# Sums of weight blocks formed by accumulating transfers instead of by VectorE additions

## The chip, the core and the metric

The kernel runs on one core of a Trainium2 chip. The core has a matrix engine (TensorE, "PE" in the profile, with its weight loads as "PEld"), a vector engine (VectorE, "DVE"), a scalar engine (ScalarE, "ACT"), GpSimd ("POOL") and SyncE ("SP"). In this kernel SP and POOL do little besides starting transfers: each has a queue of its own, works through it in order, and an entry that has to wait for something holds up all that stand behind it. The metric is the device time of one execution in microseconds (us).

## The reference

Two layers of a decoder trunk on 512 positions of width 1024, all in float32: dilated sliding-window attention, then a gated recurrent block, each followed by a gated convolutional feed-forward block. What matters here is one product of the attention layer, the values of groups 1 and 2:

```python
def dilated_attention_mixer(x, w_qkv, w_o, rel_bias):
    B, S, _ = x.shape
    qkv = (x @ w_qkv).reshape(B, S, N_GROUPS, 3, HEADS_PER_GROUP, HEAD_DIM)
    outs, lses = [], []
    for g in range(N_GROUPS):
        tbl = rel_bias[:, g * HEADS_PER_GROUP:(g + 1) * HEADS_PER_GROUP]
        o, lse = dilated_group_attention(qkv[:, :, g, 0], qkv[:, :, g, 1], qkv[:, :, g, 2],
                                         tbl, WINDOWS[g], DILATIONS[g])
```

`x` here is the normalised input, 512 x 1024, and `w_qkv` is 1024 x 9216. The bias of each head comes from a table `rel_bias` by distance.

## The kernel before

**Numbers.** A float32 product is made of three passes of TensorE: each operand is split into a high part (`hi`, rounded) and a rest (`lo = raw - hi`), and hi·hi, hi·lo and lo·hi are added up in PSUM.

**Weights.** All weights come through one list, `plan`, in the order of use. `load` (L243) starts the transfer of an entry into one of three buffers named `raw`, mostly 1 MB, on SP's queue. `pump` (L187) takes an entry apart into two units, ScalarE writes `whi` (L215) and VectorE writes `wlo` (L226, or L165 in the first entries). At most eight units may be ready or in use (`W_UNITS`). `loads` (L239) starts further entries while fewer than three buffers are unread. After each stretch of matrix work the program calls `tick`, which lets `pump` make one or two units and advances the side jobs (softmax, bias tables and the like). So on each engine the order is that of one Python program written in the order of TensorE's work; nothing reorders it later.

**Seven products.** The value projection of groups 1 and 2 is made, twice (for head pairs 0 and 1, and for 2 and 3), by seven products of half-size blocks instead of eight. Four of the seven need a sum of weight blocks as one operand. Let W(i, f) be the block of 512 rows i and 512 columns f. The list holds, for each of the two rounds, the blocks W(0,0) and W(1,0); then a first sum A = W(0,0) + W(0,1); B = A + W(1,1); C = B + W(1,0); then W(1,1) alone; then D = W(0,1) + W(1,1). Between these stand the weights of the query and key projections (`w_cols`). The entries of a sum are called `held` and `sum0` (both blocks of a fresh sum) or `sum` (one block added to the last sum):

```python
            [q("value", 0, 0), q("value", 1, 0)],
            [q("held", 0, 0), q("sum0", 0, 1)],
            [q("sum", 1, 1)],
            [q("sum", 1, 0)],
            [q("value", 1, 1)],
            [q("held", 0, 1), q("sum0", 1, 1)],
```

All go through `raw` buffers. `added` (L230) adds on VectorE, half a block at a time, into a tile `sum` that shares the place of the tile `gain` (the norms' gains); then the halves of `sum` are split into `whi` and `wlo` like any other weight. A block has 1024 column pieces of 1 KB each: 128 partitions, four rows of each, two groups' columns.

**POOL's queue.** POOL's queue carries the transfers around the bias tables. For each group g a small table `bv` is written to DRAM (`rowv`, L652) and copied from there, once per partition, to a DRAM tensor `skew` (L653, 1.5 MB). Each head then loads its bias tile `toe` from `skew` (L666); VectorE adds it to the scores (L855). Behind the third group's copy follow three constants (`e`, `back`, `res`, L658 to L660), a `toe`, and the parameter vectors of the recurrent and feed-forward layers: `columns` (L545) loads them as rows of a tile `st` (L551), and TensorE transposes them (`cols`, L554), in its own order of work between the value products of the first attention group:

```python
        for src, c in parts:
            nc.gpsimd.dma_start(st[at : at + c, :P], src)
        ps = psum("cols")
        nc.tensor.transpose(ps[:, :n], st[:n, :P], ident[:n, :n])
```

## Time and profile before

| | |
|---|---|
| median of three runs | 1480.7 us (1479.73 to 1480.92) |
| the profiled execution | 1480.85 us, span 1479.1 us |
| TensorE busy | 1466.7 us, 99% of the span |
| VectorE busy | 856.0 us, 58% |
| ScalarE busy | 623.2 us, 42% |
| GpSimd busy | 34.2 us, 2% |
| TensorE clock granted | 0.997 |

The span is the time from the first to the last recorded instruction; 1.75 us of the execution lie around it. A row of the timeline reads: start, duration, engine, line, operation, what is written and read, and in brackets how long the engine had stood idle and what ended that. A row of a group gives the count, the busy time in total, the mean of one in ns, and the idle time ahead of it with its releaser. "POOL" or "SPq" beside a DMA means that the row is the starting of a transfer; "to landing" is the time from there until its data are there.

### The profile page before, as it was taken

What the parts mean: (1) busy time and instruction counts of PE and PEld (TensorE: products, weight loads), DVE (VectorE), ACT (ScalarE), POOL (GpSimd) and SP (SyncE); (2) the same over time, 40 slices, a digit from 0 to 9 for tenths busy, and PEclk for the clock granted to TensorE, in tenths of its full rate; (3) what the DMA queues carried; (4) which work ended last, traced back from release to release, by engine and by line L of the source; (5) the groups of instructions that cost most, each with busy time, mean ns of one, the idle gap of its engine ahead of it and who ended that gap; (6) DMA issues with size and microseconds to landing.
All of it is one profiled execution on the core that took longest, in us unless ns stands there. A gap on an engine that the chain in (4) does not pass through costs nothing.

```text
span 1479.1 us, 17722 instructions
## 1 busy us (share of the span) xinstructions
PE 1466.7 (99%) x7049; PEld 1232.1 (83%) x7049; DVE 856.0 (58%) x1459; ACT 623.2 (42%) x1042; POOL 34.2 (2%) x67
## 2 busy tenths in 40 slices
PE   8999999999999999999999999999999999999998
PEld 6788888888888898888888888988898888888886
DVE  5366746684455676555565337778775555565333
ACT  5344333343435453334344234579453333333221
POOL 0121000000000000000000000000000000000000
PEclk9999999999999999999999999999999999999999
DMA  6545354636326143232223321341323232323201
GB/s 224 202 174 166 120 177 158 202 127 223 107 90 217 35 137 114 86 110 90 93 107 116 112 86 44 100 143 57 123 92 114 87 113 86 105 95 121 107 0 57
DMA packets 129714, 174.40 MB, mean 118 GB/s; under 512 B 5775, under 2 KB 108391, under 8 KB 129632
## 3 DMA queue, kind: packets, MB, share of 16 engines
q1 hardware_dynamic: 124736, 162.02, 32.7%
q0 software_dynamic: 4896, 11.26, 2.3%
q8 instruction: 55, 0.90, 0.3%
q14 instruction: 27, 0.22, 0.1%
HBM read 164.82 MB, written 13.14 MB: 120 GB/s over the span
## 4 chain that ended last, share of the span: by engine, by line
PE 97%; DVE 1%; DMA 1%; ACT 1%; SPq 0%; issue 0%; DVEq 0%
PE ps L326 59%; PE acc L326 23%; PE vq L757 5%; PE v L697 3%; PE gate L326 1%; PE tr L375 1%; PE S L932 1%; PE O L903 1%; PE S L868 1%; DMA raw<-in_attn_w_qkv_dram 1%; PE O L1000 1%; PE PT L890 0%; PE PT L981 0%; DVE wlo L226 0%; ACT L L920 0%; PE OT L1004 0%
## 5 line engine op out<-in xcount | busy, mean ns | idle before, releaser
L326 PE MATMUL ps<-hT,whi 128*128 128x512 f32 (+1 forms) x2752 | 802.0, 376 | 0.0
L326 PEld LDWEIGHTS ps<-hT,whi 128*128 128x128 f32 x2752 | 502.7, 188 | 93.1 <-ACT qk L677 0.6
L326 PE MATMUL ps<-hT,wlo 128*128 128x512 f32 (+1 forms) x1376 | 515.2, 374 | 0.0
L226 DVE TENSOR_TENSOR wlo<-raw,whi 128x1024 fp32r<-128x1024 f32 x244 | 295.5, 1219 | 130.0 <-ACT whi L215 129.5
L215 ACT ACTIVATE whi<-raw 128x1024 fp32r<-128x1024 f32 x244 | 253.2, 1052 | 136.6 <-PE acc L326 124.4
L326 PEld LDWEIGHTS ps<-hT,wlo 128*128 128x128 f32 x1376 | 259.0, 188 | 46.4
L604 DVE SCALAR_TENSOR_TENSOR u<-ps,cols,u 128x511 f32<-128x511 f32 x192 | 143.8, 749 | 217.1 <-ACT u L600 213.7
L326 PE MATMUL acc<-whi,ahi 128*128 128x512 f32 x512 | 200.4, 391 | 0.0
L326 PE MATMUL acc<-whi,alo 128*128 128x512 f32 x512 | 199.3, 389 | 0.0
L326 PE MATMUL acc<-wlo,ahi 128*128 128x512 f32 x512 | 199.2, 389 | 0.0
L600 ACT ACTIVATE u<-ps,cols 128x512 f32<-128x512 f32 x96 | 74.8, 779 | 220.0 <-PE ps L326 215.6
L326 PEld LDWEIGHTS acc<-whi,alo 128*128 128x128 f32 x512 | 96.1, 188 | 20.1
L326 PEld LDWEIGHTS acc<-wlo,ahi 128*128 128x128 f32 x512 | 96.2, 188 | 19.6
L326 PEld LDWEIGHTS acc<-whi,ahi 128*128 128x128 f32 x512 | 96.1, 188 | 19.6
L615 ACT ACTIVATE u<-u 128x512 f32<-128x512 f32 x48 | 30.4, 633 | 79.6 <-DVE u L604 79.6
L421 DVE TENSOR_TENSOR post<-acc,gain 128x512 f32<-128x512 f32 x32 | 21.8, 687 | 42.4 <-ACT junk L333 42.4
L677 ACT ACTIVATE qk<-ps 128x512 f32<-128x512 f32 x24 | 14.2, 593 | 71.4 <-PE ps L326 71.4
L855 DVE CUSTOM_DVE_ANT_0 L<-S,toe 128x128 f32<-128x128 f32 (+1 forms) x96 | 25.2, 320 | 30.4 <-PE S L868 14.7
L697 PE MATMUL v<-whi,hT 128*128 128x512 f32 x128 | 42.3, 410 | 0.3 <-ACT hT L379 0.3
L333 ACT ACTIVATE junk<-acc 128x512 f32<-128x512 f32 x32 | 19.0, 596 | 56.0 <-PE acc L326 56.0
L757 PE MATMUL vq<-whi,T 128*128 128x512 f32 x128 | 41.2, 393 | 0.0
L679 DVE COPY qk<-ps 128x512 f32<-128x512 f32 x24 | 16.5, 689 | 35.1 <-PE ps L326 35.1
(197 smaller groups left out, 1184.5 us busy)
## 6 DMA issues: line engine op xcount, KB each, us to landing
raw<-in_ffn_w_up_dram SPq DMA_DIRECT2D x48, 1024.0 KB, 5.2
raw<-in_attn_w_qkv_dram SPq DMA_DIRECT2D x26, 1024.0 KB, 5.1
raw<-in_ffn_w_down_dram SPq DMA_DIRECT2D x24, 1024.0 KB, 4.9
raw<-in_attn_w_qkv_dram SPq DMA_DIRECT2D x40, 512.0 KB, 4.5
raw<-in_lru_w_in_dram SPq DMA_DIRECT2D x8, 1024.0 KB, 5.4
skew<-rowv POOLq DMA_DIRECT2D x3, 1536.0 KB, 12.0
vp<-vrows SPq DMA_DIRECT2D x16, 256.0 KB, 7.4
raw<-in_attn_w_o_dram SPq DMA_DIRECT2D x4, 1024.0 KB, 4.9
```

The lines of the kernel that those rows point to most:

```text
L215: nc.scalar.activation(hi, raw, AF.Copy)
L226: nc.vector.tensor_tensor(lo, raw, hi.bitcast(F32), op=ALU.subtract)
L326: mm(dst, l[a], r[b], start=start and n == 0, stop=stop and n == 2)
L333: nc.scalar.activation(junk, h, AF.Square, accum_out=ss[:, i : i + 1])
L421: nc.vector.tensor_tensor(u[i], banks[i], gh[i], op=ALU.mult)
L600: nc.scalar.activation(u, ps, AF.Identity, scale=cc[:, j : j + 1], bias=cc[:, 48 + j : 49 + j])
L604: nc.vector.scalar_tensor_tensor(u[:, d:], ps[:, : S - d], wc, u[:, d:], op0=ALU.mult, op1=ALU.add)
L615: nc.scalar.activation(u, u, AF.Gelu_apprx_tanh)
L679: nc.vector.tensor_copy(dst, src)
L697: mm(banks[t], hT[a][:, k, t * P : (t + 1) * P], W[b][:, k % 2, :], start=(k, a, b) == (0, 0, 0), stop=(k, a, b) == (KD - 1, 1, 0),)
L757: mm(banks[u], act(a)[:, 2 * j + k, u * P : (u + 1) * P], W[b][:, k, :], start=(j, k, n) == (0, 0, 0), stop=(j, k, n) == (1, 1, 2),)
L855: nc.vector.tensor_tensor_reduce(dst, ps, bias, scale=1.0, scalar=3 * NEG, op0=ALU.add, op1=ALU.max, accum_out=mx)
```

## The change

The additions on VectorE are gone. A fresh sum is started by a plain transfer of its first block on SP's queue, straight into the tile `sum` (entry kind `first`); every further block is a transfer on POOL's queue that adds to what `sum` holds (`accum_op=ALU.add`). Each block is two transfers of 512 KB, one for each group's columns. Such entries take no `raw` buffer. `loads` now asks, for an entry that adds, whether the last sum is still unread (`busy`), and otherwise for a free buffer, as before. The splits into `whi` and `wlo` read the tile `sum` as before.

```diff
-        if kind == "held":
-            total["held"] = raw
+        if kind == "first":
             return []
-        if kind in ("value", "sum0", "sum"):
+        if kind in ("value", "sum"):
             return [raw[:, 2 * i : 2 * i + 2, :] for i in range(2)]
...
-                if plan[i][0] in ("sum0", "sum"):
-                    raw = added(plan[i][0], j, raw)
-                    if last:
-                        state["read"] += 1 + (plan[i][0] == "sum0")
-                        last = False
...
-    def added(kind, j, raw):
-
-        if kind == "sum0" and j == 0:
+    def done_reading(i):
+        if plan[i][0] == "sum":
+            total["busy"] = False
+        else:
+            state["read"] += 1
+
+    def loads():
+        while state["dma"] < len(plan):
+            adds = plan[state["dma"]][0] in ("first", "sum")
+            if total["busy"] if adds else state["dma"] - state["read"] >= RAW_BUFS:
+                break
+            load()
+
+    def add_up(i, kind, srcs):
+
+        if kind == "first":
             total["sum"] = cp.tile([P, 4, 512], F32, tag="gain", name=nm("sum"))
-        h = slice(2 * j, 2 * j + 2)
-        part = total["sum"][:, h, :]
-        nc.vector.tensor_tensor(part, total["held"][:, h, :] if kind == "sum0" else part, raw, op=ALU.add)
-        return part
-
-    def loads():
-        while state["dma"] < len(plan) and state["dma"] - state["read"] < RAW_BUFS:
-            load()
+        at = 0
+        for src, n in srcs:
+            dst = total["sum"][:, :, at : at + n]
+            if kind == "first":
+                nc.sync.dma_start(dst, src)
+            else:
+                nc.gpsimd.dma_start(dst, src, accum_op=ALU.add)
+            at += n
+        raws[i] = total["sum"]
+        total["busy"] = kind == "sum"
+        state["read"] += 1
+        state["dma"] += 1
...
-            [q("held", 0, 0), q("sum0", 0, 1)],
+            [q("first", 0, 0), q("sum", 0, 1)],
...
-            [q("held", 0, 1), q("sum0", 1, 1)],
+            [q("first", 0, 1), q("sum", 1, 1)],
```

In the program's order TensorE's and ScalarE's instructions are the same and in the same places; VectorE has 16 fewer. The queues change. On POOL's queue, before, from the first two heads' `toe` on (names in brackets are what an entry waits for: `DMASW` are transfers of POOL's own queue, `DMAHW` those of SP's):

```order
L666 DMA toe_669<-skew_127 128x256 [waits DMASW1_49]
L652 DMA rowv_126<-bv_725 8x384 [waits DMASW2_49,DVE_49]
L653 DMA skew_129<-rowv_126 1024x1x384 [waits DMASW3_49,DMASW2_49]
L658 DMA e_121<-in_c_e_dram 128x512 [waits PE_49]
L659 DMA back<-in_c_back_dram 128x128
L660 DMA res<-in_c_res_dram 128x8
L666 DMA toe_928<-skew_127 128x256 [waits DMASW7_49,DMASW0_49]
L551 DMA st_989<-in_lru_conv_w_dram 8x128
```

The same place after the change:

```order
L681 DMA toe_669<-skew_127 128x256 [waits DMASW1_49]
L249 DMA sum_697<-in_attn_w_qkv_dram 128x4x256 [waits DMAHW5_49,DMAHW2_49,DMASW2_49]
L249 DMA sum_697<-in_attn_w_qkv_dram 128x4x256 [waits DMAHW6_49,DMASW3_49]
L667 DMA rowv_126<-bv_730 8x384 [waits DVE_49]
L668 DMA skew_129<-rowv_126 1024x1x384 [waits DMASW4_49]
L673 DMA e_121<-in_c_e_dram 128x512 [waits PE_49]
L674 DMA back<-in_c_back_dram 128x128 [waits DMASW7_49]
L675 DMA res<-in_c_res_dram 128x8 [waits DMASW0_49]
L681 DMA toe_929<-skew_127 128x256 [waits DMASW1_49]
L566 DMA st_986<-in_lru_conv_w_dram 8x128 [waits DMASW2_49]
```

The two adding transfers of the first sum stand ahead of `rowv`, the third `skew` copy, the constants, the `toe` of head 2 and the parameter rows, and each waits for one of SP's transfers. On SP's queue, before, around the same point of the program (`raw_784` is the `held` block):

```order
L253 DMA raw_576<-in_attn_w_qkv_dram 128x4x512 [waits DMAHW7_49,DMAHW6_49,DVE_49]
L253 DMA raw_695<-in_attn_w_qkv_dram 128x8x256 [waits DMAHW1_49,DMAHW0_49,DVE_49]
L253 DMA raw_784<-in_attn_w_qkv_dram 128x4x256 [waits DMAHW2_49,DVE_49]
L253 DMA raw_784<-in_attn_w_qkv_dram 128x4x256
L784 DMA vrows_580<-v_844 128x512 [waits DVE_49]
```

And after:

```order
L268 DMA raw_576<-in_attn_w_qkv_dram 128x4x512 [waits DMAHW7_49,DMAHW6_49,DVE_49]
L268 DMA raw_695<-in_attn_w_qkv_dram 128x8x256 [waits DMAHW1_49,DMAHW0_49,DVE_49]
L247 DMA sum_697<-in_attn_w_qkv_dram 128x4x256 x2
L268 DMA raw_789<-in_attn_w_qkv_dram 128x8x256 [waits DMAHW2_49,DVE_49]
L799 DMA vrows_580<-v_848 128x512 [waits DVE_49]
```

The first block now waits for nothing of VectorE; the weights of the next projection take its former place. Later on POOL's queue, the adding transfers of B, C and D of the first round stand ahead of the `toe` loads of heads 4 and 5, and those of A, B and C of the second round ahead of the first `toe` loads of groups 1 and 2.

More of the change, by code (lines that the diff above doesn't have):

```diff
@@ L170 @@
     sides, first_tiles = [], []
-    total = {}
+    total = {"busy": False}
     def parts_of(kind, raw):
@@ L212, in pump @@
                         split(hi[c], lo[c], raw[c])
-                    state["read"] += last
+                    if last:
+                        done_reading(i)
                 else:
@@ L224, in low_parts @@
     def low_parts():
-        for _, _, lo, raw, hi, last in late:
+        for i, _, lo, raw, hi, last in late:
             nc.vector.tensor_tensor(lo, raw, hi.bitcast(F32), op=ALU.subtract)
-            state["read"] += last
+            if last:
+                done_reading(i)
         late.clear()
-    def added(kind, j, raw):
-        if kind == "sum0" and j == 0:
-            total["sum"] = cp.tile([P, 4, 512], F32, tag="gain", name=nm("sum"))
-        h = slice(2 * j, 2 * j + 2)
-        part = total["sum"][:, h, :]
-        nc.vector.tensor_tensor(part, total["held"][:, h, :] if kind == "sum0" else part, raw, op=ALU.add)
-        return part
-    def loads():
-        while state["dma"] < len(plan) and state["dma"] - state["read"] < RAW_BUFS:
-            load()
+    def done_reading(i):
[11 more added lines that the diff above has]
+        if kind == "first":
+            total["sum"] = cp.tile([P, 4, 512], F32, tag="gain", name=nm("sum"))
+        at = 0
[10 more added lines that the diff above has]
+        state["dma"] += 1
     def load():
@@ L245, in load @@
         kind, kd, cols, srcs = plan[i]
+        if kind in ("first", "sum"):
+            return add_up(i, kind, srcs)
         raw = wp.tile([P, kd, cols], F32, tag="raw", name=nm("raw"), bufs=RAW_BUFS)
```

## The prediction

> **What bounds the kernel now.** I read the page's busy times and chain first, then busy time by stretch, then TensorE's waits in the stage of the change.

> ```profile
> span 1479.1 us, 17722 instructions
> PE 1466.7 (99%) x7049; PEld 1232.1 (83%) x7049; DVE 856.0 (58%) x1459; ACT 623.2 (42%) x1042; POOL 34.2 (2%) x67
> ...
> PE 97%; DVE 1%; DMA 1%; ACT 1%; SPq 0%; issue 0%; DVEq 0%
> ```

> TensorE is busy for 99% of the span and is 97% of the chain that ended last. By stretch (columns: length, then busy time and count of PE, PEld, DVE, ACT, POOL, then granted clock, DMA share, GB/s):

> ```profile
> 90.00:115.00 25.00, 25.00 (x134) 21.49 (x134) 14.80 (x25) 9.87 (x18) 11.53 (x22) 1.00 0.75 261
> 115.00:135.00 20.00, 20.00 (x96) 16.39 (x95) 12.94 (x41) 10.12 (x23) 1.98 (x4) 1.00 0.54 175
> 250.00:345.00 95.00, 95.00 (x462) 79.97 (x461) 63.78 (x116) 37.95 (x72) 2.15 (x4) 1.00 0.51 167
> ```

> In the stage of the change TensorE has no gap and the full clock. TensorE's matrix queue waits for nothing between 100 and 345 us; its weight loads have this one row:

> ```profile
> PEld cols L554 <- issue: 0.4, 1, 0.4
> ```

> So time can be won only outside of what the change touches, and it can be lost wherever TensorE is made to wait, since nothing later has slack to give it back.

> **What is removed.** The groups of the additions, and of ScalarE's splits that read them:

> ```profile
> L215 ACT ACTIVATE whi<-sum 128x1024 fp32r<-128x1024 f32 x16 | 16.9, 1058 | 33.7 <-DVE sum L236 33.7
> ...
> L236 DVE TENSOR_TENSOR sum<-raw,raw 128x1024 f32<-128x1024 f32 x8 | 9.8, 1221 | 0.5 <-DMA raw<-in_attn_w_qkv_dram 0.5
> L236 DVE TENSOR_TENSOR sum<-sum,raw 128x1024 f32<-128x1024 f32 x8 | 9.7, 1218 | 0.0
> ```

> 16 additions of 1.22 us are 19.5 us of VectorE; ScalarE idled 33.7 us for them. Both lie beside TensorE's matrix work, and no wait of TensorE follows from them, so they are worth 0 on the path. The bound above is the one 0.4 us wait. The raw buffers that the sums no longer take let other weights come earlier; TensorE waits for no weight here, so 0 as well.

> **What is added at the first sum.** This is where I put the cost. SP's queue, and the landing of weights that start together (first the 1 MB of `raw_695` alone; then, at 269 us, two halves of 512 KB and 1 MB behind them):

> ```profile
> 88.69 0.37 SPq L253 DMA_DIRECT2D raw<-in_attn_w_qkv_dram  x1
> 96.74 0.98 SPq L253 DMA_DIRECT2D raw<-in_attn_w_qkv_dram  x2
> ...
> 269.37 1.49 SPq L253 DMA_DIRECT2D raw<-in_attn_w_qkv_dram  x3
> ```

> ```profile
> raw<-in_attn_w_qkv_dram SPq DMA_DIRECT2D x1, 1024.0 KB, 4.8
> ...
> raw<-in_attn_w_qkv_dram SPq DMA_DIRECT2D x2, 512.0 KB, 4.1
> raw<-in_attn_w_qkv_dram SPq DMA_DIRECT2D x1, 1024.0 KB, 7.5
> ```

> The block that was `held` started at 96.74, when a raw buffer came free. It now waits for no buffer and follows `raw_695` at once, near 89.1. The third row of 269 starts about 0.9 us behind the first and takes 7.5, so two megabytes end 8.4 us after the first start: 3.6 us for the second one. The first half of W(0,0) then lands at 88.69 + 4.8 + 1.8 = 95.3, the second at 97.1. Each releases one adding transfer on POOL's queue. POOL stands still meanwhile, and behind it stand these (start times before):

> ```profile
> 91.14 0.53 POOL L652 DMA_DIRECT2D rowv<-bv  x1 [21.74 <-DVE bv L651]
> 93.97 1.12 POOL L653 DMA_DIRECT2D skew<-rowv  x1 [2.30 <-DMA rowv<-bv]
> ...
> 96.69 0.56 POOL L666 DMA_DIRECT2D toe<-skew  x1
> ```

> ```profile
> 105.80 0.51 POOL L551 DMA_DIRECT2D st<-in_lru_conv_w_dram  x1 [7.05 <-DMA skew<-rowv]
> ...
> 108.19 0.51 POOL L551 DMA_DIRECT2D st<-in_lru_lambda_dram  x1
> ```

> It is a serial chain: `rowv` must land before `skew` starts, the fourth parameter row waits until `skew` has landed (105.80 - 93.97 = 11.8 us), and the last one, lambda, starts 2.4 us later. Whatever delays the start of `skew` delays lambda as much. Lambda's landing, and TensorE's transpose that needs it:

> ```profile
> st<-in_lru_lambda_dram POOLq DMA_DIRECT2D x1, 4.0 KB, 5.5
> ```

> ```profile
> 118.39 0.27 PE L554 MATMUL cols<-ident,st 64*128 64x64 f32 x1
> ```

> Lambda landed at 108.19 + 5.5 = 113.7; TensorE came to the transpose at 118.4. The slack is 4.7 us. It works in order, so any further delay of the chain is a stall of all matrix work.

> How long the adding transfers take no row shows. The nearest are plain transfers on POOL's queue, and the queue's behaviour behind a long one:

> ```profile
> gain<-in_norm_ffn_post_dram POOLq DMA_DIRECT2D x1, 512.0 KB, 3.8
> gain<-in_norm_mix_pre_dram POOLq DMA_DIRECT2D x1, 512.0 KB, 4.8
> ```

> ```profile
> skew<-rowv POOLq DMA_DIRECT2D x1, 1536.0 KB, 12.0
> toe<-skew POOLq DMA_DIRECT2D x2, 128.0 KB, 11.1
> ```

> ```profile
> 79.63 0.29 DVE L855 CUSTOM_DVE_ANT_0 L<-S,toe 128x128 f32<-128x128 f32 x1 [13.56 <-DMA toe<-skew]
> ```

> The two `toe` loads started right behind a `skew` copy took 11.1 us, as long as the copy; the page's median for sixteen half as large is 2.1:

> ```profile
> toe<-skew POOLq DMA_DIRECT2D x16, 64.0 KB, 2.1
> ```

> So POOL's transfers land in order, and `rowv` will land behind the adding pair. (That wait cost VectorE 13.56 us and TensorE none.) Lower end for the pair: plain price. The second half starts at 97.1 and lands 3.8 later, at 100.9. Upper end: the rate of the `skew` copy, 8 us for a megabyte, doubled because an addition also reads its destination: 16 us. I take the plain price with the moving part doubled, being nearest to the `gain` rows in size: 3.8 is 2.0 fixed and 1.8 of moving, so 5.6 for one half and 3.6 more for the second. Call T the time from the first half's start to the second's landing: T = 9.2. The pair ends at 95.3 + 9.2 = 104.5; `skew` starts 0.3 later (my allowance for `rowv`), at 104.8, which is 10.8 later than before. Lambda lands at 124.5, and TensorE stalls 124.5 - 118.4 = **6.1 us**. In general the stall is T - 3.1.

> [...]

> **What else stands behind POOL's queue.** The `toe` of head 2 started at 96.69, and at 10.8 later it lands about 118; VectorE stands until then, as it did for 13.56 us above, with TensorE in no need of it before the transpose at which it stalls anyway. The later sums, from the timeline of VectorE and TensorE:

> ```profile
> 164.33 1.22 DVE L226 TENSOR_TENSOR wlo<-sum,whi 128x1024 fp32r<-128x1024 f32 x1
> ...
> 176.89 0.28 DVE L855 CUSTOM_DVE_ANT_0 L<-S,toe 128x128 f32<-128x128 f32 x1
> ```

> ```profile
> 269.26 2.50 DVE L226 TENSOR_TENSOR wlo<-sum,whi 128x1024 fp32r<-128x1024 f32 x2
> ...
> 290.18 0.28 DVE L855 CUSTOM_DVE_ANT_0 L<-S,toe 128x128 f32<-128x128 f32 x1
> ...
> 296.86 1.29 DVE L968 TENSOR_TENSOR L<-L,s 128x512 f32<-128x512 f32 x2
> ```

> ```profile
> 314.37 1.03 PE L981 MATMUL PT<-ident,L 128*128 128x128 f32 x8
> ```

> Times here are on the old scale; a stall at 118 shifts all alike. In the first round D's first block may start when C is split, at 165.5, lands near 170 (4.1 and a little), and the pair behind it at 179; the `toe` of head 4 comes with it, so VectorE, which wanted it at 176.9, waits some 2 us. In the second round B's pair starts at 271.8 and lands T later; two splits of 1.06 and a last subtraction of 1.22 follow, so C's pair starts at 275.1 + T and lands at 275.1 + 2T, with the first `toe` of the strided heads behind it: 293.5 for T = 9.2, where 290.2 is wanted. From the scores to the scaled weights it took 298.2 - 290.2 = 8.0 us, so TensorE's transposes at 314.4 have their input at 301.5. That costs nothing, until 283.1 + 2T passes 314.4, at T = 15.6. It is the tightest of these places.

> On SP's queue D's first block waits until VectorE has split C, and the weights behind it wait too. They did before, from the waits of SP's queue:

> ```profile
> SPq L253 <- DVE wlo L226: 1169.7, 121, 34.6
> ```

> Weight loads stood 1169.7 us behind VectorE's subtractions, up to 34.6 at once, with TensorE unaffected, so this costs 0; if that cover were gone, TensorE would wait for a weight, which it does nowhere between 100 and 345 us.

> **The sum.** The profiled execution took 1480.85 us (0.15 over the median of the runs): 1480.85 + 6.1 = **1487.0 us**, 0.4% slower. About 0.2% (3.0 us) is what a measurement of this kernel can tell from no change.

> **The rivals.** First, *the transfers are hidden after all*: no change. The stall is 1.8 us if `rowv` passes the pair in the queue (its start moves from 91.14 to 97.1 plus 0.56, 6.5 later, less 4.7), and 2.5 at the plain price: 1482.7 to 1483.4. It decides where T stays under 6.1. For it speaks that SP's plain loads of 1 KB pieces are as fast as POOL's 4 KB ones; against it the order of landing in the `toe` rows and the double reading.

> Second, *the adding transfers are slow*, T over 15.6. Then the first stall grows beyond 12.5, and TensorE also waits for the strided heads at 314, 2 us for each further one of T. At T = 20: 16.9 + (323.1 - 314.4 = 8.7) = 25.6, or 1506.5. For it speaks the `skew` rate; nothing but the half-size `gain` rows speaks against it.

> Third, *VectorE's relief shows*: faster by over 3 us. That needs idle time of TensorE between 90 and 345 us, of which there is 0.4; the time would be 1480.4, and a larger gain has no place to come from.

> **How the numbers follow.** Forecast, T from 6.1 to 15.6, that is 1483.9 to 1493.3: 0.50. First rival: 0.19. Second: 0.25. Third: 0.03. A stall at a place that I haven't seen, 3 us or more: 0.03. Faster 0.03; within 0.2% 0.19; slower 0.50 + 0.25 + 0.03 = 0.78. The range runs from 1482.0, taking in the upper half of the first rival, to 1507, T = 20: about 8 in 10. The likeliest case's own range is 1483.9 to 1493.3.

> **What would show it.** Right: POOL's first two rows of `sum` wait near 90 to 97 for a DMA of SP's, `rowv` starts near 98 and `skew` near 105, and TensorE's first row of L554 stands near 124 behind an idle gap of about 6 us, released by the `st` rows; the groups of L236 are gone, VectorE's busy time is near 836.5; VectorE has waits on `toe` near 112, 177 and 290 (later by the stall), and TensorE has none at its transposes of L981. Wrong: landing times of the adding pairs under 6 or over 15.6 us; a wait of TensorE anywhere else; or a first row of L554 without a gap.

## The result and the profile after

The changed kernel takes 1498.8 us (median of four, 1497.3 to 1499.6); the kernel before, beside it, 1480.8 (1479.7 to 1481.1). The ratio is 1.0122, with a 95% interval of 1.0104 to 1.0139: 18 us slower, where 6.1 were forecast. The profiled executions lie 16.5 us apart (1497.34 against 1480.85), and the accounts below are made against these (the one of the changed kernel is the fastest of its four).

First the page's span, busy times and chain of the changed kernel:

```profile
span 1495.6 us, 17684 instructions
PE 1471.1 (98%) x7049; PEld 1233.2 (82%) x7049; DVE 836.8 (56%) x1443; ACT 621.5 (42%) x1042; POOL 55.4 (4%) x83
...
PE 89%; DMA 5%; DVE 3%; ACT 1%; issue 1%; POOL 1%; SPq 0%; DVEq 0%; POOLq 0%; ACTq 0%
```

VectorE has lost 19.2 us of work, and nothing is gained by it. TensorE's idle time (span less busy) has grown from 12.4 to 24.5 us, by 12.1. Its busy time has grown as well, by 4.4 us, with the same 7049 instructions. Both together are the 16.5.

The idle part, in the waits of TensorE (what was waited for, then the sum, the count and the longest in us):

```profile
PE cols L569 <- DMA st<-in_lru_lambda_dram: 8.3, 1, 8.3
PE PT L996 <- DVE qk L694: 2.4, 1, 2.4
...
PE c L1001 <- ACT PT L998: 1.3, 1, 1.3
...
PE ps L341 <- DVE qk L694: 0.3, 1, 0.3
```

There are two stalls: 8.3 us at the transpose of the parameter rows, and 2.4 + 1.3 + 0.3 = 4.0 us at the transposes of the strided heads. The first in POOL's and TensorE's timelines (start, length, then in brackets the idle time before it and its releaser):

```profile
94.49 2.74 POOL L249 DMA_DIRECT2D sum<-in_attn_w_qkv_dram  x2 [26.07 <-DMA sum<-in_attn_w_qkv_dram]
96.69 1.08 POOL L667 DMA_DIRECT2D rowv<-bv  x1
108.69 1.16 POOL L668 DMA_DIRECT2D skew<-rowv  x1 [10.92 <-DMA rowv<-bv]
...
123.65 0.51 POOL L566 DMA_DIRECT2D st<-in_lru_lambda_dram  x1
```

```profile
125.73 0.34 PE L569 MATMUL cols<-ident,st 64*128 64x64 f32 x1 [8.26 <-DMA st<-in_lru_lambda_dram]
```

`rowv` stands behind the adding pair, `skew` waits 10.92 us for it, and lambda comes 15.5 us later than before. The second stall, in VectorE's timeline and then TensorE's:

```profile
310.37 0.29 DVE L870 CUSTOM_DVE_ANT_0 L<-S,toe 128x128 f32<-128x128 f32 x1 [5.29 <-DMA toe<-skew]
...
332.33 0.68 DVE L694 COPY qk<-ps 128x512 f32<-128x512 f32 x1
```

```profile
330.13 0.60 PE L996 MATMUL PT<-ident,L 128*128 128x128 f32 x4
...
333.16 0.63 PE L996 MATMUL PT<-ident,L 128*128 128x128 f32 x4 [2.43 <-DVE qk L694]
335.04 0.60 PE L1001 MATMUL c<-s,back 128*128 128x16 f32 x2 [1.26 <-ACT PT L998]
335.93 1.22 PE L341 MATMUL ps<-hT,whi 128*128 128x512 f32 x2 [0.28 <-DVE qk L694]
```

The scores of the first strided head start at 310.37, VectorE then works with one gap of 0.75 us, and its copy of `qk` at 332.33 comes too late for the second half of a group of transposes.

The busy part is the clock. Busy time by stretch around both stalls (columns as in the prediction; the third number from the end is the granted clock):

```profile
100.00:115.00 15.00, 15.00 (x86) 13.15 (x86) 4.27 (x5) 4.18 (x6) 4.85 (x8) 1.00 0.83 207
115.00:122.90 7.90, 2.47 (x11) 1.70 (x10) 0.00 (x1) 0.00 (x0) 1.25 (x3) 0.99 0.77 285
122.90:129.70 6.80, 3.97 (x11) 3.25 (x12) 4.61 (x17) 4.55 (x12) 5.80 (x12) 0.50 0.28 72
129.70:135.00 5.30, 5.30 (x27) 4.34 (x25) 4.86 (x26) 1.04 (x5) 0.00 (x0) 1.00 0.00 0
327.00:334.50 7.50, 4.36 (x23) 3.31 (x21) 7.43 (x8) 2.00 (x3) 2.87 (x4) 1.00 0.94 151
334.50:341.30 6.80, 5.97 (x15) 4.71 (x16) 6.66 (x13) 4.79 (x8) 0.00 (x0) 0.50 0.87 261
341.30:347.00 5.70, 5.70 (x27) 4.70 (x26) 3.56 (x4) 1.55 (x2) 0.00 (x0) 1.00 0.76 250
```

From 122.8 us on, while TensorE still waited for lambda, and from 334.4 on, the granted clock is 0.50 for 6.8 us each. These stretches cost more than the 4.4 us, because the execution of the changed kernel was 1.0 us ahead before it came to either stall: the first `vq` row behind a group of transposes starts at 89.99 in it and at 90.97 in the kernel before, whose granted clock between 10 and 17 us was 0.55 where the changed kernel had 1.00. TensorE's rows stand 9.2 us later behind the first stall, and 16.5 later behind the second. So the first stall cost 10.2 us, of which 8.3 are the wait and 1.9 the half clock; the second cost 7.3, of which 4.0 are waits and 3.3 the half clock. The pair of matmuls at 335.93 took 1.22 us where such pairs took 0.61 or 0.62 in the kernel before (the row of 303.49 there). Between 30 and 420 us the kernel before shows no stretch below full clock.

What the result leaves to be shown: that POOL's queue makes the first stall, what makes the second, whether the half clock is a consequence of the pauses or of the adding transfers, and why the pairs took longer than forecast.

### The profile page after: what moved, and what is told of

The parts are those of the page before. It is cut to its first block, busy times and chain, and to the rows that moved or that the text cites. A ratio compares the mean times of both kernels' runs of the same rounds, so it can differ in the third digit from the quotient of the medians.

```text
span 1495.6 us, 17684 instructions
## 1 busy us (share of the span) xinstructions
PE 1471.1 (98%) x7049; PEld 1233.2 (82%) x7049; DVE 836.8 (56%) x1443; ACT 621.5 (42%) x1042; POOL 55.4 (4%) x83
## 4 chain that ended last, share of the span: by engine, by line
PE 89%; DMA 5%; DVE 3%; ACT 1%; issue 1%; POOL 1%; SPq 0%; DVEq 0%; POOLq 0%; ACTq 0%
PE ps L341 55%; PE acc L341 23%; PE vq L772 3%; PE v L712 2%; PE gate L341 1%; DMA sum<-in_attn_w_qkv_dram 1%; DMA toe<-skew 1%; DVE wlo L221 1%; PE tr L390 1%; DMA e<-in_c_e_dram 1%; DMA rowv<-bv 1%; PE O L1015 1%; DMA raw<-in_attn_w_qkv_dram 1%; PE O L918 1%; PE S L883 1%
## 5 line engine op out<-in xcount | busy, mean ns | idle before, releaser
L221 DVE TENSOR_TENSOR wlo<-raw,whi 128x1024 fp32r<-128x1024 f32 x244 | 294.9, 1218 | 132.6 <-ACT whi L210 132.1
L341 PEld LDWEIGHTS acc<-whi,ahi 128*128 128x128 f32 x512 | 96.1, 188 | 19.6
L341 PEld LDWEIGHTS acc<-wlo,ahi 128*128 128x128 f32 x512 | 96.2, 188 | 19.5
L436 DVE TENSOR_TENSOR post<-acc,gain 128x512 f32<-128x512 f32 x32 | 21.8, 685 | 42.4 <-ACT junk L348 42.4
L692 ACT ACTIVATE qk<-ps 128x512 f32<-128x512 f32 x24 | 14.2, 592 | 75.1 <-PE ps L341 74.6
L694 DVE COPY qk<-ps 128x512 f32<-128x512 f32 x24 | 16.5, 688 | 39.4 <-PE ps L341 39.3
## 6 DMA issues: line engine op xcount, KB each, us to landing
raw<-in_ffn_w_up_dram SPq DMA_DIRECT2D x48, 1024.0 KB, 5.2
raw<-in_attn_w_qkv_dram SPq DMA_DIRECT2D x26, 1024.0 KB, 7.3
raw<-in_ffn_w_down_dram SPq DMA_DIRECT2D x24, 1024.0 KB, 4.9
raw<-in_attn_w_qkv_dram SPq DMA_DIRECT2D x16, 512.0 KB, 6.0
sum<-in_attn_w_qkv_dram POOLq DMA_DIRECT2D x16, 512.0 KB, 9.5
raw<-in_lru_w_in_dram SPq DMA_DIRECT2D x8, 1024.0 KB, 5.3
skew<-rowv POOLq DMA_DIRECT2D x3, 1536.0 KB, 12.3
sum<-in_attn_w_qkv_dram SPq DMA_DIRECT2D x8, 512.0 KB, 5.4
```

Source lines behind the costliest of these rows:

```text
L221: nc.vector.tensor_tensor(lo, raw, hi.bitcast(F32), op=ALU.subtract)
L341: mm(dst, l[a], r[b], start=start and n == 0, stop=stop and n == 2)
L436: nc.vector.tensor_tensor(u[i], banks[i], gh[i], op=ALU.mult)
L694: nc.vector.tensor_copy(dst, src)
```

## The experiments

All times are medians, each with its ratio to the kernel before measured beside it, and the 95% interval; the run with loads held was executed once. I call the four sums of a round A, B, C and D, those of the second round A' to D'.

### One round at a time

The kinds of the quarters are chosen by round; the old addition is put back for the other round:

```diff
+        one, two, more = ("first", "sum", "sum") if p0 in (0,) else ("held", "sum0", "sumv")
...
-            [q("first", 0, 0), q("sum", 0, 1)],
...
+            [q(one, 0, 0), q(two, 0, 1)],
...
```

The first run accumulates in the first round only, the second (with `p0 in (2,)`) in the second only.

> Sums of the first round by accumulating transfers, those of the second round by VectorE as before. Theory of two stalls (in the changed kernel TensorE waits 8.3 us at the transposes of the parameter rows and runs at half clock for 6.8 us after it, about 2 us more; it waits again some 4 us at the strided heads' transposes near 333 us, with about 3 us for the clock): only the first stall remains, so 1480.8 + 8.3 + 2 = 1491 us, and the half clock stands once, right after it. Rival, a loss spread over all pairs of accumulating transfers (four of eight here): half of the 18 us, 1490 us, but then the wait at the parameter rows would be shorter than 8.3 us and the missing time would lie between 130 and 345 us; the place tells them apart, not the total.

> Sums of the second round by accumulating transfers, those of the first round by VectorE as before. Theory of two stalls: no wait of TensorE at the parameter rows; the stall of about 4 us at the transposes of the strided heads, and the half clock after it (3 us), remain: 1480.8 + 7 = 1488 us. Rival (the second stall is a consequence of the first, since the delayed first round shifts VectorE's and the loads' order): no stall at the strided heads, 1481 us. Rival for the clock (the half clock comes from the load of the accumulating transfers, not from a pause of TensorE): a half clock also where TensorE had not paused.

The first round alone: 1491.8 us, 1.0078 (1.0063 to 1.0093). The second alone: 1488.4 us, 1.0054 (1.0039 to 1.0069). Together 11.5 + 8.1 = 19.6 us over the before of those runs, near the 18 of the whole change. The waits of TensorE, of the first run and then of the second:

```profile
PE cols L586 <- DMA st<-in_lru_lambda_dram: 9.1, 1, 9.1
```

```profile
PE PT L1013 <- DVE qk L711: 2.4, 1, 2.4
...
PE c L1018 <- ACT PT L1015: 0.8, 1, 0.8
```

Each run keeps its stall and shows nothing of the other; the half clock lasted 10.2 us in the first run and 6.8 in the second, each at its stall. The two stalls are independent, and the loss sits at two places, not in all pairs.

### The first sum's pair further back in POOL's queue

A list keeps the adding transfers of chosen sums back, and they are started at a later point of the program:

```diff
-                nc.gpsimd.dma_start(dst, src, accum_op=ALU.add)
+                waiting.append((dst, src))
...
+        if kind == "sum":
+            state["sums"] += 1
+            if state["sums"] not in HOLD:
+                flush()
```

With `HOLD = (1,)` only A's pair is held; with `(1, 4, 7)` also D's, meant to go behind the `toe` loads of heads 4 and 5, and that of C', meant to go behind the first strided `toe` loads.

> Only the first sum's pair of accumulating transfers is moved on POOL's queue: it is issued behind rowv, skew, the parameter rows and lambda, instead of ahead of rowv. All other pairs stay. If the place in POOL's queue makes the first stall, TensorE's wait of 8.3 us at the parameter rows goes, and the half clock behind it; the second stall stays: 1498.8 - 10.3 = 1488.5 us. Rival (the pair delays the parameter rows by taking the DMA engines, wherever it stands in the queue, or the sum that now lands later delays TensorE through its own splits): little is won, 1494 us or more, with the wait moved to another transfer or to the matmuls on the sum.

> Three pairs are moved behind on POOL's queue: the first sum's behind lambda as in the run before; the fourth sum's of the first round behind the toe loads of heads 4 and 5; the third sum's of the second round behind the first toe loads of the strided heads. If the second stall comes from the toe loads that stand behind a pair, it goes too: 1480.8 to 1483 us, and no half clock between 100 and 345 us. Rival (the second stall comes from the sums being late for ScalarE's splits, with VectorE's work piling up behind them): it stays or grows, 1488 us or more.

The first gave 1493.5 us, 1.0091 (1.0076 to 1.0106): about 5 us won, not 10. The second gave 1493.9, 1.0096 (1.0079 to 1.0113), no better. TensorE still waits at the parameter rows, 3.4 us in the first and 3.5 in the second. The profile of the first names a `toe` transfer as the releaser, but POOL's timeline of the first of the two shows what was late:

```profile
98.75 0.54 POOL L696 DMA_DIRECT2D toe<-skew  x1
99.27 2.74 POOL L246 DMA_DIRECT2D sum<-in_attn_w_qkv_dram  x2
...
110.23 0.55 POOL L580 DMA_DIRECT2D st<-in_lru_conv_w_dram  x1 [7.68 <-DMA skew<-rowv]
...
114.61 0.50 POOL L580 DMA_DIRECT2D st<-in_lru_gx_b_dram  x1 [1.39 <-DMA sum<-in_attn_w_qkv_dram]
118.45 0.51 POOL L580 DMA_DIRECT2D st<-in_lru_lambda_dram  x1 [3.34 <-DMA sum<-in_attn_w_qkv_dram]
```

The pair had gone behind `rowv`, `skew` and one `toe`, but not behind the parameter rows: the split of A stands ahead of these in the program and forces the pair out. And `gx_b` and lambda wait for the sum, though they have nothing to do with it. In this program a transfer of POOL's starts only when the eighth one before it has landed: `gx_b` is the eighth after the pair's first half, lambda the eighth after the second. In the same way the parameter row that is the eighth behind `skew` waits for `skew`: 7.68 us here, and 7.05 in the kernel before, where it is the fourth row. So the move was not the clean test that I meant; the sum still stood in lambda's way, by another door.

In both runs the second stall is unchanged (2.4 + 1.3 us). The second of them decides nothing about it either: the split of C' stands ahead of the strided `toe` loads in the program, and forced its pair out first (295.03, the `toe` loads 296.53). Only D's pair was moved, and that changed nothing that TensorE waits for. Whether the `toe` loads behind the pair of C' make the second stall had to be asked in another way (below).

### Parameter rows and toe out of the way

The eight parameter rows get a tile of their own and are loaded right after the first `skew` copy; the rest is the changed kernel:

```diff
...
+                if g == 0:
+                    early_rows()
                 yield 3
```

and in a second run A's pair is moved as above as well, so that the `toe` load of head 2 is ahead of it.

> The changed kernel, with the eight parameter rows (conv, gates, lambda) loaded right after the first skew copy near 52 us, into a tile of their own, instead of behind the third one. Lambda then waits for no sum. If the chain through POOL's queue to lambda is all that makes the first stall, the 8.3 us and the half clock behind it go: 1488.5 us. Rival (the toe load of head 2, which stands behind the pair as well and landed at 122.9, is next: VectorE waits for it with the weights' splits queued behind, due at TensorE about 2 us after the parameter rows): a stall of 4 to 6 us at the matmuls behind the parameter rows, 1492 to 1496 us.

> The parameter rows early as in the run before the last, and the first sum's pair also behind rowv, skew and the toe load of head 2. Nothing that TensorE or VectorE needs before 125 us stands behind the pair any more. If POOL's queue makes the first stall, all of it goes and only the second round's stall stays: 1488 us. Rival (the sum itself, landing near 118 behind the skew copy, is now late for its splits): a stall between 120 and 130 us, 1490 us or more, released by a split of the sum.

The rows alone won almost nothing: 1497.0 us, 1.0113 (1.0098 to 1.0128). The stall only moved, and it came out later than the rival had put it. In VectorE's and TensorE's timelines of that run:

```profile
124.76 0.29 DVE L884 CUSTOM_DVE_ANT_0 L<-S,toe 128x128 f32<-128x128 f32 x1 [17.41 <-DMA toe<-skew]
```

```profile
127.31 0.28 PE L570 MATMUL cols<-ident,st 96*128 96x96 f32 x1 [1.17 <-DMA st<-in_ffn_conv_b_dram]
134.92 1.23 PE L919 MATMUL PT<-ident,L 128*128 128x128 f32 x7 [1.65 <-DVE s L884]
139.24 1.22 PE L341 MATMUL ps<-hT,whi 128*128 128x512 f32 x2 [3.08 <-ACT v L741]
```

VectorE still stood 17.4 us for the `toe` load of head 2 behind the same pair, and TensorE met the consequences at three places, 5.9 us, with 6.8 us of half clock.

With both out of the way the first stall is gone: 1489.7 us, 1.0061 (1.0046 to 1.0076), full clock from 30 to 320 us, and no wait of TensorE over 0.6 us between 100 and 320. The waits that are left are the second stall's:

```profile
PE PT L1028 <- DVE qk L722: 2.4, 1, 2.4
PE c L1033 <- ACT PT L1030: 1.3, 1, 1.3
```

So the place in POOL's queue makes the first stall. Two chains hang on it, not one, and the second (`toe`, then VectorE) is nearly as late as the first.

### First round put right, second by VectorE; and one sum less in series

Both start from the last kernel. In one the second round's sums are made by VectorE. In the other only C' is, from a raw buffer, so that one pair instead of two stands between the splits of A' and the strided `toe` loads:

```diff
-            [q("sum", 1, 0)],
+            [q("sumv" if p0 == 2 else "sum", 1, 0)],
```

> The first round with its sums by accumulating transfers, parameter rows early and the first sum's pair behind the toe load of head 2, as in the run in which the first stall went; the second round's sums by VectorE as before. If the two stalls and the half clock behind each are the whole loss, nothing is left: 1480.5 to 1482.5 us, the same as the kernel before. Rival (the accumulating transfers also cost something spread over the first round): 1484 us or more.

> As in the run in which the first stall went, and of the second round's sums the third alone is made by VectorE again, from a raw buffer, so that only one pair in place of two stands between the splits of the second round's first sum and the toe load of the strided heads. If the two pairs in series (16 and 10 us), with ScalarE's and VectorE's work queued in order behind them, make the second stall, it goes: 1481 to 1483 us and no half clock between 100 and 345 us. Rival (the first of the two pairs, 16 us, is enough, or the backlog comes from elsewhere): a stall of some 2 to 4 us stays near 320 us, 1486 to 1489 us.

The first gave 1481.2 us, 1.0002 (0.9993 to 1.0011): the same as the kernel before. Four accumulated sums with nothing urgent behind them cost nothing, and the 9.5 us less of VectorE's work win nothing. The second gave 1482.1 us, 1.0010 (1.0001 to 1.0020), with seven of eight sums accumulated. Neither shows a half clock between 30 and 420 us. Pages of the first and the second:

```profile
span 1479.6 us, 17701 instructions
PE 1467.0 (99%) x7049; PEld 1232.0 (83%) x7049; DVE 846.5 (57%) x1451; ACT 622.3 (42%) x1042; POOL 44.7 (3%) x75
```

```profile
span 1480.0 us, 17692 instructions
PE 1467.0 (99%) x7049; PEld 1231.9 (83%) x7049; DVE 838.8 (57%) x1445; ACT 621.8 (42%) x1042; POOL 53.0 (4%) x81
```

So the second stall is made by the two pairs in series: 15.9 us for B' (start at 279.89, split at 295.76 in the changed kernel) and 10.4 for C' (299.61 to 310.01), with the `toe` loads and VectorE's work behind them in order. (C' by an accumulating transfer with B' by VectorE was not run.) The slow pair alone is just covered: in the last run VectorE's copy of `qk` starts at 319.40, 5.6 us later than in the kernel before, and TensorE waits 0.4 and 0.5 us.

### A pause without any accumulating transfer

The kernel before, in which POOL is kept busy right ahead of the third `rowv` transfer:

```diff
+                if g == 2:
+                    fill = cp.tile([P, P], F32, tag="fill", name="fill")
+                    nc.gpsimd.tensor_copy(fill[:8, :], bv[:8, :P])
+                    for _ in range(FILL):
+                        nc.gpsimd.memset(fill, 0.0)
                 nc.gpsimd.dma_start(rowv[g], bv[:8, :TOE])
```

> The kernel before, sums by VectorE, without any accumulating transfer; POOL is kept busy for about 13 us with memsets of a spare tile right ahead of the third rowv transfer, so that skew, toe and lambda come about as late as in the changed kernel. If the half clock is the consequence of TensorE's pause, TensorE stalls about 8 us at the parameter rows and runs at half clock for 3.4 to 10.3 us after it, in steps of 3.4 as in the four runs before: 1480.5 + 8 + 2 = 1490.5 us for a delay of 13 us (one us more or less with the delay). Rival (the half clock comes from the adding transfers' load): the same stall at full clock, 1488.5 us.

The delay came out as 19.2 us instead of 13 (`rowv` starts at 110.34, 91.14 before). TensorE waited 10.6 us for lambda and the time was 1493.8 us, 1.0092 (1.0077 to 1.0107). By stretch:

```profile
110.00:123.50 13.50, 8.35 (x45) 6.89 (x43) 0.00 (x0) 1.04 (x2) 5.54 (x11) 1.00 0.56 193
123.50:133.50 10.00, 4.53 (x12) 3.71 (x13) 6.25 (x21) 4.55 (x12) 7.62 (x15) 0.51 0.25 69
133.50:140.00 6.50, 6.50 (x30) 5.32 (x30) 5.88 (x26) 2.84 (x10) 0.54 (x1) 0.97 0.70 204
```

The half clock is there, for 10.2 us, in a kernel without adding transfers. It is a consequence of TensorE's pause. The span grew by 12.9 us: 10.6 are the wait, and 2.3 are left for the half clock.

### What sets the length of a pair

Three runs: plain transfers in place of the adding ones (`accum_op=ALU.add` left out, so the additions of the blocks are not made); a sum that counts as a raw buffer until it is split; and no load of SP's started while a pair isn't yet split:

```diff
-            if total["busy"] if adds else state["dma"] - state["read"] >= RAW_BUFS:
+            if total["busy"] or not adds and state["dma"] - state["read"] >= RAW_BUFS:
```

(the last of them; the second had `adds and total["busy"] or ...`, and took a slot in the count for each sum).

> The changed kernel with each of the sixteen adding transfers replaced by a plain one of the same block from the same queue at the same place: the additions of the blocks are left out, and the output is that of overwritten sums. It prices the adding itself. If the double work of an addition sets a pair's time, as the prediction assumed (plain 3.8 us for one half of 512 KB, and twice the moving part with the addition), a plain pair takes 5 to 7 us beside SP's loads and 4 to 6 alone, against 13.5 to 16 and 8.7; the first stall falls under 3 us and the second goes: 1482 to 1485 us. Rival (the pairs are slow because they share the DMA engines with SP's loads, adding or not): plain pairs of 10 us and more at the same places, 1493 us or more.

> The changed kernel, in which a sum counts as one of the raw buffers until it has been split, so that SP's queue starts fewer weight loads beside an adding pair. In the changed kernel the pairs with a megabyte or two of SP's loads beside them took 13.5 to 16 us from the first start to the second landing, one with nothing beside it 8.7. If the loads beside them are the cause, the first sum's pair takes about 9 and TensorE's first stall falls from 8.3 to about 4, the second round's slow pair takes about 10 and its stall of 4 us goes: 1485 to 1489 us. Rival (the adding transfers are slow by themselves, or by what else stands at that place): pairs and stalls stay as they are, 1497 to 1499 us.

> The changed kernel, in which no weight load of SP's queue is started as long as an adding pair has not been split; the pairs have the DMA engines nearly to themselves, and the weights behind them come later, which may make TensorE wait for weights (so its total time is not what is asked). If SP's loads beside the pairs lengthen them, the first sum's pair falls from 13.5 us to about 9 (first start to second landing) and the one that took 16 to 9 to 10, and lambda's wait from 8.3 to about 4 us. Rival (an adding pair takes that long by itself at these places): 13 us and more as before.

The run with loads held is the clean one for A, whose pair starts at the same place with the same work around it, but no megabyte of SP's beside it. It took 1610.6 us, since TensorE then waits for weights; that is not what was asked. The landing times of A's two halves (the first alone, then the median of both; the last number, in us), in the changed kernel:

```profile
sum<-in_attn_w_qkv_dram POOLq DMA_DIRECT2D x1, 512.0 KB, 9.5
...
sum<-in_attn_w_qkv_dram POOLq DMA_DIRECT2D x2, 512.0 KB, 10.8
raw<-in_attn_w_qkv_dram SPq DMA_DIRECT2D x1, 1024.0 KB, 9.3
```

with the loads held, the median of both and the first, and the end of the wait for `rowv`:

```profile
sum<-in_attn_w_qkv_dram POOLq DMA_DIRECT2D x2, 512.0 KB, 7.0
...
sum<-in_attn_w_qkv_dram POOLq DMA_DIRECT2D x1, 512.0 KB, 6.3
```

```profile
104.69 1.16 POOL L668 DMA_DIRECT2D skew<-rowv  x1 [6.44 <-DMA rowv<-bv]
...
120.40 0.24 PE L569 MATMUL cols<-ident,st 64*128 64x64 f32 x1 [2.48 <-DMA st<-in_lru_lambda_dram]
```

and as plain transfers, with the loads beside them, the first half and the second:

```profile
sum<-in_attn_w_qkv_dram POOLq DMA_DIRECT2D x1, 512.0 KB, 4.9
...
sum<-in_attn_w_qkv_dram POOLq DMA_DIRECT2D x1, 512.0 KB, 7.6
```

From the first half's start to the second's landing that makes (the second half starts 1.4 us behind the first, and twice the median less the first is its landing time): adding beside loads 1.4 + 12.1 = 13.5 us; adding alone 1.4 + 7.7 = 9.1; plain beside loads 1.4 + 7.6 = 9.0. Adding and sharing each cost about 4.5 us here. The pair that landed with a median of 13.1 us in the changed kernel (B', beside a 1 MB load that took 15.2) landed with 6.9 in the run with loads held, where only two loads started earlier were still landing, the last of them 3.4 us behind its start. Lambda's wait fell to 2.5 us, below the 4 expected.

Where the two shared, both sides got slower: A's pair took half as long again beside SP's megabyte (13.5 us against 9.1), which itself took 9.3 us, where a megabyte alone took 4.8.

The plain run as a whole gave 1487.5 us, 1.0043 (1.0028 to 1.0058), between what the two theories expected: the second stall is gone (TensorE waits for nothing there), the first is 3.8 us, with 6.8 us of half clock from its last microsecond on. So neither the addition nor the sharing alone explains the first stall; it takes both to reach 8.3.

The run in which a sum takes a slot decided nothing: 1496.9 us, 1.0114 (1.0097 to 1.0131). It moved A's pair behind `skew` as a side effect, and beside the pair of B' three of SP's loads still ran (its split waited 21.8 us, as before).

## Why the prediction was wrong, point by point

**What bounds the kernel, and the additions worth nothing: right.** The kernel with the first round put right saves half of the additions and measures 1.0002. VectorE's busy time fell to 836.8, forecast 836.5.

**The place and mechanism of the first stall: right.** The pair ahead of `rowv` on POOL's queue, `skew` behind `rowv`, lambda behind `skew`, TensorE's gap released by the `st` rows: all as described, and the two runs with parameter rows and `toe` moved show it.

**The size of T at the first sum: too small, by a cost left out.** The prediction took 9.2 us, plain price with the moving part doubled. Alone, the pair measured 9.1, and the plain pair at B's place 5.5, with no load of SP's beside it, so that price was right. (Its split of 3.8 us into 2.0 fixed and 1.8 of moving, of which the second was doubled, is an estimate that no run shows, and so is the reason given for the doubling, that an addition also reads its destination; the smaller transfers of POOL's queue in the kernel before landed with medians of 1.8 us for the 12 KB of `rowv` and 2.1 for the 64 KB of `toe`.) It had priced the transfer alone, though, and not beside the 1 MB load `raw_789`, which SP's queue now starts at 95.33, since the sums no longer take raw buffers. The prediction named that earlier start ("other weights come earlier") and put it at 0. With it T is 13.5. The stall came out at 8.3 and not at 13.5 - 3.1 = 10.4, because another term erred the other way: lambda landed 1.9 us after its issue, where the prediction carried over 5.5. That takes off 3.6; smaller terms give 1.5 back, above all that TensorE was 1.0 us ahead, and that lambda was issued 15.0 us behind `skew` instead of 14.2. That the stall came so near to the forecast is in part luck.

**The second round: the wrong place was taken for the tightest.** The forecast was no wait here until 283.1 + 2T passes 314.4. The two pairs took 15.9 + 10.4 = 26.3 us, less than twice 15.6, and yet TensorE stalled 4 us. The first transposes had the slack that was forecast, and did not wait. But VectorE works in order, and behind these scores it also copies `qk` out of a PSUM bank that the next transposes need. In the kernel before, VectorE's and TensorE's rows there are

```profile
313.85 0.68 DVE L679 COPY qk<-ps 128x512 f32<-128x512 f32 x1
```

```profile
320.94 1.03 PE L981 MATMUL PT<-ident,L 128*128 128x128 f32 x8
```

The copy ends at 314.5; the second half of these transposes, 0.6 us into the group, is due at 321.5. That is 7.0 us of slack, not the 12.9 between 301.5 and 314.4. TensorE's group stands 9.2 us later in the changed kernel (330.13), so the copy was due by 323.0 without a delay of its own; it came at 332.33, 9.3 late. 9.3 - 7.0 = 2.3 us, and the wait is 2.43. (With one sum less in series the copy was 5.6 late, which is under 7.0, and this wait was gone.) (ScalarE's and VectorE's next pieces add the 1.3 and 0.3.)

**The clock: left out altogether.** The prediction counted a stall at its length. Each stall brought 6.8 us of half clock, which cost 1.9 us at the first and 3.3 at the second.

The account of the profiled execution: 6.1 forecast; 2.2 more at the first stall (8.3); 4.0 at the second; 5.2 by the clock; less the 1.0 that it was ahead from its start. That is the 16.5 measured.

**The rivals.** The first (hidden, T under 6.1) fell: even alone the pair took 9.1. The third fell. The second foresaw stalls at both places, with T over 15.6 as the price of adding. Both stalls came, but not by that price: of the changed kernel's pairs only B' reached it (15.7 us from the first start to the second landing), and only beside SP's loads; A's pair took 13.5. A stall at a place not seen, which had 0.03, is what came in part: the place was on the list, the wait for the `qk` copy was not.

**Signs announced.** `rowv` near 98 (started at 96.69), the gap in front of the first `cols` row, VectorE's waits on `toe`: as announced. `skew` near 105: it started at 108.69, by the longer pair. "None at the transposes": wrong, and by the prediction's own list that shows the second round's step to be at fault. B', at 15.7 us, is just over the 15.6 that was named as a sign of being wrong.

## What to carry to other kernels

Price a transfer beside what its queue neighbours will start in the same microseconds (A's pair took 9.1 us alone and 13.5 beside 1 MB); an edit that frees buffers makes those start earlier. Look for slack not at the first reader of a late result, but at everything that the engine holding it does next in order, down to the first thing that TensorE needs. And where TensorE is the bound, a pause can be paid for twice: once as the wait, and again at half clock. Here 8.3 us of waiting cost 1.9 more and 4.0 us cost 3.3 more: 2.9 us of the first stall's half clock still lay in the wait. (A pause of 3.5 us, with A and D moved, brought none.) The waits of 2.43, 1.26 and 0.28 us that stand close together at the second stall brought the same 6.8 us of half clock as the one of 8.3.

## What the runs showed of the hardware

**The clock after a pause.** The length of TensorE's pause, and of the half clock that began in it or behind it: 3.4 us of pause, 3.4 us of half clock (A's pair moved); 3.5, none (A and D moved); 3.8, 6.8 (plain); 6.4, 6.8 (a sum takes a slot); 8.3, 6.8 (the change); 9.1, 10.2 (first round only); 10.6, 10.2 (POOL kept busy). All the half clocks are multiples of 3.4 us, and pauses of 3.4 and 3.5 us went either way. With loads held, a pause of 2.5 us was enough for 3.4 us of half clock, and at the second stall of the changed kernel no pause was longer than 2.43 us.

The transposes counted as busy time here: in the kernel before, the window from 19.69 to 23.10 us holds 2.60 us of busy time, of which eight transposes make 1.3, and the clock stayed at 1.00 behind it. Without them 1.3 would be left, less than the 1.48 below which it never stayed.

**Adding transfers.** 512 KB added to SBUF from POOL's queue took POOL 1.3 us to issue and 5.8 to 6.3 us to land for the first of a pair alone. That is about 2 us more than a plain one (4.0 to 4.1 us for the first half where no other load ran beside it, and 0.75 to issue).

**Eight at a time.** In this program a transfer on POOL's queue waits until the eighth before it has landed, so that a slow one holds up two places: right behind it, and eight further on (`gx_b` 1.4 us and lambda 3.3, in the run with A's pair moved).
